# Attention scores: the low part of the queries in both halves of a tile

## The chip, the cores and the metric

The kernel runs on one core of a Trainium2 chip. The metric is the device time of one launch in microseconds. The kernel before takes 2771.27 us, the median of 3 runs (2769.14 to 2774.12).

Five engines work side by side, each through its own instructions in order, and wait for each other by semaphores: TensorE (PE; the load of its stationary operand stands in the profile as an engine of its own, PEld), VectorE (DVE), ScalarE (ACT), GpSimd (POOL) and SyncE (SP). PE writes to PSUM, the others work on SBUF and PSUM.

## What is computed

Two layers of a model over 512 latent and 256 context tokens of width 1024. In each layer a normed input goes through one projection and then through three mixers side by side (neighbourhood attention, a gated delta rule, a Fourier transform), whose results are gated, merged and projected; an MLP follows. The change lies in the attention, 8 heads of width 64:

```python
s_loc = (jnp.einsum('bwhd,biwjhd->bhwij', q_r, k_win).astype(jnp.float32)
         + jnp.transpose(bias, (0, 2, 1, 3)).astype(jnp.float32)[None])
s_ctx = jnp.einsum('bwhd,bshd->bhws', q_r, kc).astype(jnp.float32)
s = jnp.concatenate([s_loc.reshape(b, h, GRID_W, kh * kw), s_ctx], axis=-1)
p = jax.nn.softmax(s, axis=-1).astype(v.dtype)
...
return (jnp.einsum('bhwij,biwjhd->bwhd', p_loc, v_win)
        + jnp.einsum('bhws,bshd->bwhd', p[..., kh * kw:], vc))
```

In layer 0 the context tokens attend to each other as well.

## The kernel before

**Tiling.** Activations lie feature-major, 128 features on the partitions and up to 768 tokens along them. Products are made of two float32r parts each: a weight or an activation is its rounded part (`hi`) plus the remainder (`lo`), and `proj` (L240) adds up hi x hi, hi x lo and lo x hi over eight groups of 128 features, in pieces of 512 and 256 tokens. Weights come from memory by `wload` (L225): SP issues the transfer, ACT rounds, POOL or DVE makes the remainder.

**Attention.** Heads are treated in pairs, since two heads of 64 features fill 128 partitions. `na_in` (L745) makes three projections for a pair. Of the keys it keeps, for each head, a tile `ks` whose one half holds the rounded part of the head's keys and whose other half holds their remainder (L753 to L756). Of the queries it makes, for each head, a tile `qd` with the rounded part in both halves (ACT writes the one, DVE the other, L778 and L779), and for both heads one tile `qlo` with the remainder, each head in its own half (DVE, L780).

`na_attn` (L823) goes over the query tiles of a pair, 128 queries each: four local ones and, in layer 0, two of the context. `score` (L826) makes the scores of one head by two products into one PSUM bank: L829 takes `qd` against `ks` over 128 rows (rounded queries with both parts of the keys), L830 takes `qlo` against the rounded keys, over the 64 rows of that head. A local tile has 256 local and 256 context keys; its local keys are one piece of 256 columns, and two of 128 columns in the first tile. So a pair has 22 products with `qlo` in layer 0 and 18 in layer 1, and the kernel 160.

`na_pair` (L784) does the rest for both heads: DVE takes the maximum and adds the bias (L793, L796), ACT takes the exponentials (L800, L803), DVE divides (L807), PE transposes the weights (L812), ACT copies them (L813), and PE multiplies by the values (L818).

**Order.** Within the stage of the mixers four streams are emitted side by side by clocks of their own (`by_clock`, L330): the scan of the delta rule (`dn_step`), its preparation (`dn_prep`, with a chain of 31 x 2 small DVE steps, L581 and L583, that inverts blocks), the attention, and the projections with the gates (`stream_in`). A scheduler then sets each engine's order from the order of emission, as priority, and from an estimate of when each operand is there. The order is fixed in the program: on the chip an engine waits at an instruction whose operands are late, and all behind it waits too. Projections are what PE does between the steps of the other streams.

**Room.** The tiles of a stage lie in pools, each tag with a number of buffers in rotation. `ks`, `qd`, `qlo`, the values and the output share the tag `n` with 7 buffers, as many as one pair uses (L1044).

Of the kernel before, what the change touches and what calls it, by code (L numbers as in the profile page):

```python
# [9 lines left out]
F32 = mybir.dt.float32  # L10
# [17 lines left out]
# n-tiles of w_in, 128 columns each  # L28
T_NAK, T_NAV, T_NAQ, T_DNK, T_DNV, T_DNQ, T_Z, T_U, T_GATE = 0, 4, 8, 12, 16, 20, 24, 28, 32
# PSUM buffers of the mixers; buffers of the raw and of the split weights  # L30
PSX = {"pl": 2, "pa": 1, "ch": 2, "s": 2, "pp": 1}
WRAW, WSPLIT, WADA = 4, 3, 8
# order in which the streams of the mixers are emitted, for each layer: the share of the clock that a projection and
# a step of the scan take, the lead and the priority of the scan, the gates per projection and those ahead of it
IN_T, LAT_STEP, HEAD, PRI, GR, G0 = (12, 7), (2, 3), (5, 0), (200, 0), (0.5, 0.3), (0, 1)
# rows of adaLN tiles per projection, and how far their loads run ahead
ADA_RATE, ADA_LAG = 0.6, 1
# gates computed beside the mixers
NPRE = 16
# columns of the vector block  # L40
# [4 lines left out]
def kernel(ctx: ExitStack, tc: tile.TileContext, A: dict, out: bass.AP):  # L45
# [75 lines left out]
    def sigmoid_into(dst, src):  # L121
        """exp(min(x, 0) - log(1 + exp(-|x|))); dst is not src"""
        act.activation(out=dst, in_=src, func=AF.Abs)
        act.activation(out=dst, in_=dst, func=AF.Exp, scale=-1.0)
        act.activation(out=dst, in_=dst, func=AF.Ln, bias=1.0)
        dve.scalar_tensor_tensor(dst, in0=src, scalar=0.0, in1=dst, op0=ALU.min, op1=ALU.subtract)
        act.activation(out=dst, in_=dst, func=AF.Exp)

# [9 lines left out]
    def ada_block(l, q):  # L138
        """columns 512*q .. 512*q+511 of the adaLN projection of layer l, the contraction in four column groups"""
# [16 lines left out]
    def ada_group(l, q, lag):  # L156
        """four such blocks from the one at q, one in each column group; loads run lag rows of tiles ahead"""
# [26 lines left out]
    def ada_scale(l, i, k0=0, n=KD):  # L184
        """norm weight * (1 + scale) of the norm i of layer l"""
# [27 lines left out]
    def ada_upto(l, q):  # L213
        """what follows needs the block q of layer l"""
# [8 lines left out]
    wcnt = [0]  # L223

    def wload(src, kn=KD):  # L225
        """[P, kn, 128] float32 -> for each k two float32r parts whose sum is the float32 one"""
# [13 lines left out]
    def proj(ps, w, kn, xh, xl, segs, off=0, k0=0, k1=KD):  # L240
        """ps[:, seg - off] = sum_k w[:, k].T @ x[k][:, seg], of it the part from k0 to k1"""
# [6 lines left out]
    def split_act(src, w, name, alloc):  # L248
        """float32 SBUF tile -> (hi, lo) tiles"""
# [7 lines left out]
    class Rms:  # L257
        """1 / rms of each token; the last of the tiles goes straight to the sum over partitions"""
# [33 lines left out]
    def mod_norm(l, i, xs, w, nm):  # L292
        """the modulated norm as two parts"""
# [24 lines left out]
    def modulate(k, x):  # L318
        """the first modulation, of a normalised tile that is no longer needed"""
# [10 lines left out]
    def by_clock(pri, *streams):  # L330
        """merge generators that yield the time of what they have emitted, by their clocks"""
# [33 lines left out]
    def layer(l):  # L365
# [39 lines left out]
        def gates():  # L405
# [40 lines left out]
            # rows of the summed log-decays, for a broadcast over partitions  # L446
# [7 lines left out]
        odn = drp.tile([NDH, P, TT], F32, tag="odn", bufs=1, name="odn")  # L454

        def conv_silu(ps, cw, w):
            """short conv over tokens and silu; the result at [0:512] and [514:770]"""
# [41 lines left out]
        def tok_major(src, offs, name, tag):  # L499
            """[feature, token] -> [token, 6, feature]"""  # L500
# [23 lines left out]
        def dn_prep(h, st):  # L524
# [41 lines left out]
            # inverses of the 32x32 diagonal blocks, one block on each partition  # L566
# [28 lines left out]
            # merge 32 -> 64  # L595
# [23 lines left out]
            # merge 64 -> 128  # L619
# [26 lines left out]
        def dn_step(h, st, d, step):  # L646
            """one chunk of the scan of direction d"""
# [95 lines left out]
        ona = drp.tile([4, P, TT], F32, tag="ona", bufs=1, name="ona")  # L743

        def na_in(c, st):  # L745
            # scores as products of two parts each: the two halves of a stack hold the parts of one head
# [26 lines left out]
            if full:  # L773
                act.activation(out=raw[:, TL:TT], in_=ps[1][:, 0:TC], func=AF.Copy, scale=0.125)
            qd = [U("qd", F32R, tag="n") for _ in range(2)]
            qlo = U("qlo", F32R, tag="n")
            for t, r, r2 in zip(qd, halves, halves[::-1]):
                act.copy(t[r, :W], raw[r, :W])  # L778
                dve.tensor_copy(t[r2, :W], raw[r, :W])  # L779
                dve.tensor_tensor(qlo[r, :W], raw[r, :W], t[r, :W].bitcast(F32), op=ALU.subtract)  # L780
            st.update(ks=ks, vt=vt, qd=qd, qlo=qlo)
            yield IN_T[l]

        def na_pair(scores, n_loc, biases, vts, dst, view):  # L784
            """softmax over the keys of 128 queries for both heads of a pair; the outputs to dst, feature-major"""
# [37 lines left out]
        def na_attn(c, st):  # L823
            vt = st["vt"]

            def score(ps, hh, q0, k0, n):  # L826
                r = slice(64 * hh, 64 * hh + 64)
                q, k = slice(q0, q0 + P), slice(k0, k0 + n)
                pe.matmul(ps, lhsT=st["qd"][hh][:, q], rhs=st["ks"][hh][:, k], start=True, stop=False)  # L829
                pe.matmul(ps, lhsT=st["qlo"][r, q], rhs=st["ks"][hh][r, k], start=False, stop=True)  # L830
# [40 lines left out]
        ofn = drp.tile([4, P, TT], F32, tag="ofn", bufs=1, name="ofn")  # L871

        def fourier():
# [34 lines left out]
            for i, (s0, n, tab) in enumerate(sets):  # L908
# [24 lines left out]
                for g in range(4):  # L933
# [9 lines left out]
                    else:  # L943
                        # the transform at (n - t, -f) is the one at (t, f); -f lies 64 rows away, but for 0 and 64
# [36 lines left out]
        def stream_na():  # L981
            for c, st in enumerate(nas):
                while "qlo" not in st:
# [60 lines left out]
        mix_b = scope("mixb", n=7, N=1, PT=2, L=1, pr=3, sp=7, S=3, s6=6, Pm=2, bias=2, stmp=1)  # L1044
# [67 lines left out]
        for hb in range(4):  # L1112
# [12 lines left out]
            for k in range(KD):  # L1125
# [3 lines left out]
                # the last one in halves of the tokens, so that the final norm starts early  # L1129
# [165 lines left out]
```

## Time and profile before

| | |
|---|---|
| time, median of 3 runs | 2771.27 us |
| span of the profiled execution, first to last instruction | 2750.2 us |
| time around the span (median less span) | 21.1 us |
| PE busy | 2618.0 us, 95% |
| DVE busy | 1391.2 us, 51% |
| ACT busy | 1191.1 us, 43% |
| mixers of layer 0 | 145 to 772 us of the span |
| mixers of layer 1 | 1687 to 2218 us of the span |

The profiled execution is one run; its own time is not listed apart from its span, so the median less the span is taken for what lies around it. The busy time of an engine is the union of its instructions' intervals. PE's products are pipelined and their intervals overlap, so the step of PE's work is read from one start to the next, not from the durations.

### The profile page before, as it was taken

To read this page: it belongs to the slowest core of one execution; us is meant where nothing else is said; L and a number is where in the kernel's file an instruction comes from. 1 tells how busy PE (TensorE), PEld (TensorE's weight loads), DVE (VectorE), ACT (ScalarE), POOL (GpSimd) and SP (SyncE) were. 2 spreads that over 40 slices of the span, in tenths; PEclk is the share of its full clock that TensorE was granted. 3 is DMA by queue.
4 is the path that set the end of the run, shared out by engine and by line. 5 is a ranking of instruction groups with operands and counts; after the bars stand their busy time and mean duration, and the time that the engine had idled before them with its cause. 6 is when DMAs were issued, how large, how long until landed. Compare 5 with 4: busy or idle time off the path is not lost.

```text
span 2750.2 us, 40072 instructions
## 1 busy us (share of the span) xinstructions
PE 2618.0 (95%) x15066; PEld 2103.9 (77%) x15066; DVE 1391.2 (51%) x2831; ACT 1191.1 (43%) x2430; POOL 609.1 (22%) x522
## 2 busy tenths in 40 slices
PE   6999999999999999999999988998999999999998
PEld 3877768677878777888888867776777777788886
DVE  5657576857423634222222365768677436433334
ACT  4546555555543224121222255455565654423333
POOL 3222212231111112111111123221323222222222
PEclk9999999999999999999999999999999999999999
DMA  6232222221255743342312223232232335333332
GB/s 219 81 87 68 78 58 75 71 71 53 68 197 189 255 139 115 104 135 91 120 59 66 81 60 111 72 81 58 79 85 63 93 112 187 96 95 96 96 96 88
DMA packets 196705, 278.41 MB, mean 101 GB/s; under 512 B 56768, under 2 KB 75936, under 8 KB 196512
## 3 DMA queue, kind: packets, MB, share of 16 engines
q1 hardware_dynamic: 196512, 275.87, 32.9%
q8 instruction: 118, 1.93, 0.3%
q14 instruction: 75, 0.61, 0.1%
HBM read 244.29 MB, written 27.31 MB: 99 GB/s over the span
## 4 chain that ended last, share of the span: by engine, by line
PE 73%; DVE 8%; ACT 3%; DMA 1%; issue 1%; POOL 1%; SPq 0%; DVEq 0%; ACTq 0%; POOLq 0%
PE ps_m L245 32%; PE ps_in L245 14%; PE ps_br L245 6%; PE ps_wo L245 4%; PE ps_inc L245 3%; PE ps_ada L168 1%; DVE cy L468 1%; PE ps_s L830 1%; PE ps_s L818 1%; PE ps_s L829 1%; PE ps_s L812 1%; DVE xn L303 1%; PE ps_ch L676 1%; DVE stmp L581 1%; DMA Db<-gdr 1%
## 5 line engine op out<-in xcount | busy, mean ns | idle before, releaser
L236 POOL TENSOR_TENSOR wlo<-wr,whi 128x512 fp32r<-128x512 f32 x360 | 484.8, 1348 | 1894.7 <-ACT whi L233 1789.7
L233 ACT CAST whi<-wr 128x512 fp32r<-128x512 f32 x560 | 346.3, 619 | 879.9 <-PE ps_m L245 519.8
L245 PE MATMUL ps_in<-hh,whi 128*128 128x512 f32 x960 | 381.0, 408 | 11.8 <-ACT kraw L750 5.5
L245 PE MATMUL ps_in<-hh,wlo 128*128 128x512 f32 x960 | 378.2, 404 | 2.2 <-POOL wlo L236 2.2
L245 PE MATMUL ps_in<-hl,whi 128*128 128x512 f32 x960 | 377.7, 404 | 0.0
L236 DVE TENSOR_TENSOR wlo<-wr,whi 128x512 fp32r<-128x512 f32 x200 | 138.6, 693 | 244.7 <-ACT whi L233 243.9
L245 PE MATMUL ps_m<-ml,whi 128*128 128x512 f32 (+1 forms) x768 | 233.8, 358 | 4.1 <-POOL ml L313 3.2
L245 PE MATMUL ps_m<-mh,whi 128*128 128x512 f32 (+1 forms) x768 | 233.0, 358 | 2.9 <-ACT mh L309 2.9
L245 PE MATMUL ps_m<-ah,wlo 128*128 128x512 f32 (+1 forms) x776 | 234.4, 355 | 0.0
L245 PE MATMUL ps_m<-ah,whi 128*128 128x512 f32 (+1 forms) x776 | 234.2, 355 | 0.0
L245 PE MATMUL ps_m<-al,whi 128*128 128x512 f32 (+1 forms) x776 | 233.2, 353 | 0.0
L245 PE MATMUL ps_m<-mh,wlo 128*128 128x512 f32 (+1 forms) x768 | 231.7, 355 | 0.0
L245 PEld LDWEIGHTS ps_in<-hh,whi 128*128 128x128 f32 x960 | 181.8, 194 | 48.1 <-ACT kraw L750 5.9
L245 PEld LDWEIGHTS ps_in<-hh,wlo 128*128 128x128 f32 x960 | 181.2, 193 | 36.5 <-POOL wlo L236 3.4
L245 PEld LDWEIGHTS ps_in<-hl,whi 128*128 128x128 f32 x960 | 181.4, 194 | 32.8 <-issue 2.0
L1134 DVE SCALAR_TENSOR_TENSOR x<-ps_m,mod,x 128x512 f32<-128x512 f32 (+1 forms) x97 | 60.8, 655 | 247.8 <-PE ps_m L245 247.8
L245 PEld LDWEIGHTS ps_m<-mh,whi 128*128 128x128 f32 x768 | 126.6, 189 | 35.3 <-ACT whi L233 8.4
L245 PEld LDWEIGHTS ps_m<-ah,whi 128*128 128x128 f32 x776 | 127.7, 188 | 28.9 <-ACT whi L233 6.7
L245 PE MATMUL ps_inc<-hh,whi 128*128 128x256 f32 x512 | 149.6, 292 | 0.0
L245 PEld LDWEIGHTS ps_m<-ml,whi 128*128 128x128 f32 x768 | 126.8, 188 | 29.5 <-POOL ml L313 6.0
L245 PE MATMUL ps_inc<-hl,whi 128*128 128x256 f32 x512 | 148.7, 290 | 0.0
L245 PE MATMUL ps_inc<-hh,wlo 128*128 128x256 f32 x512 | 147.0, 287 | 0.0
(325 smaller groups left out, 4927.3 us busy)
## 6 DMA issues: line engine op xcount, KB each, us to landing
wr<-in_w_dram SPq DMA_DIRECT2D x256, 256.0 KB
wr<-in_wi_dram SPq DMA_DIRECT2D x224, 256.0 KB
wada<-in_wa_dram SPq DMA_DIRECT2D x192, 256.0 KB
wr<-in_wb_dram SPq DMA_DIRECT2D x48, 256.0 KB
wr<-in_wo_dram SPq DMA_DIRECT2D x32, 256.0 KB
gpre<-sgp SPq DMA_DIRECT2D x16, 384.0 KB
sgg<-gpre SPq DMA_DIRECT2D x16, 384.0 KB
rot<-kn SPq DMA_DIRECT2D x64, 64.0 KB
```

The costliest lines, as they stand in the source:

```text
L168: pe.matmul(ps[32 * j:32 * j + 32, :], lhsT=cs[:, k, :], rhs=ws[k][j], start=(k == 0), stop=(k == KD - 1), tile_position=(0, 32 * j))
L233: act.copy(hi, raw)
L236: eng.tensor_tensor(lo, raw, hi.bitcast(F32), op=ALU.subtract)
L245: pe.matmul(ps[:, s0 - off:s1 - off], lhsT=a, rhs=b[k][:, s0:s1], start=(k == 0 and i == 0), stop=(k == kn - 1 and i == 2))
L303: dve.scalar_tensor_tensor(t[:, s0:s1], in0=xs[k][:, s0:s1], scalar=sc, in1=rs[:, s0:s1], op0=ALU.mult, op1=ALU.mult)
L468: dve.scalar_tensor_tensor(y[:, :n], in0=cin[:, j:j + n], scalar=vec[:, cw + j:cw + j + 1], in1=y[:, :n], op0=ALU.mult, op1=ALU.add)
L581: dve.tensor_tensor(tv, Nb[:, j + 1:32, j:j + 1].to_broadcast([48, n, m]), Wb[:, j:j + 1, 0:m].to_broadcast([48, n, m]), op=ALU.mult)
L676: pe.matmul(ps[:, 2 * P:3 * P], lhsT=kt, rhs=Uc, start=True, stop=True)
L812: pe.transpose(ps[:, i * P:(i + 1) * P], Pm[:, i * P:(i + 1) * P], ident)
L818: pe.matmul(pss[0][f, 0:P], lhsT=v[:, f], rhs=Pt[:, i * P:(i + 1) * P], start=(i == 0), stop=(i == nk // P - 1), tile_position=(0, 64 * hh))
L829: pe.matmul(ps, lhsT=st["qd"][hh][:, q], rhs=st["ks"][hh][:, k], start=True, stop=False)
L1134: dve.scalar_tensor_tensor(x2[k][:, s0:s1], in0=ps[:, s0:s1], scalar=mod(l, 5, k, v), in1=x2[k][:, s0:s1], op0=ALU.mult, op1=ALU.add)
```

## The change

`qlo` is replaced by two tiles `ql`, one for each head, that hold the remainder of the head's queries in both halves. DVE makes both halves by a subtraction each. The second score product then runs over 128 rows like the first: remainder of the queries against both parts of the keys. So it also adds the product of the two remainders, which was left out before. The tag `n` gets an eighth buffer, and the space for descriptors of dynamic transfers is set to 2048 bytes. Comments are removed, which moves the line numbers.

```diff
             qd = [U("qd", F32R, tag="n") for _ in range(2)]
-            qlo = U("qlo", F32R, tag="n")
-            for t, r, r2 in zip(qd, halves, halves[::-1]):
+            ql = [U("ql", F32R, tag="n") for _ in range(2)]
+            for t, lo, r, r2 in zip(qd, ql, halves, halves[::-1]):
                 act.copy(t[r, :W], raw[r, :W])
                 dve.tensor_copy(t[r2, :W], raw[r, :W])
-                dve.tensor_tensor(qlo[r, :W], raw[r, :W], t[r, :W].bitcast(F32), op=ALU.subtract)
-            st.update(ks=ks, vt=vt, qd=qd, qlo=qlo)
+                for x in (r, r2):
+                    dve.tensor_tensor(lo[x, :W], raw[r, :W], t[r, :W].bitcast(F32), op=ALU.subtract)
+            st.update(ks=ks, vt=vt, qd=qd, ql=ql)
...
             def score(ps, hh, q0, k0, n):
-                r = slice(64 * hh, 64 * hh + 64)
                 q, k = slice(q0, q0 + P), slice(k0, k0 + n)
                 pe.matmul(ps, lhsT=st["qd"][hh][:, q], rhs=st["ks"][hh][:, k], start=True, stop=False)
-                pe.matmul(ps, lhsT=st["qlo"][r, q], rhs=st["ks"][hh][r, k], start=False, stop=True)
+                pe.matmul(ps, lhsT=st["ql"][hh][:, q], rhs=st["ks"][hh][:, k], start=False, stop=True)
...
-        mix_b = scope("mixb", n=7, N=1, PT=2, L=1, pr=3, sp=7, S=3, s6=6, Pm=2, bias=2, stmp=1)
+        mix_b = scope("mixb", n=8, N=1, PT=2, L=1, pr=3, sp=7, S=3, s6=6, Pm=2, bias=2, stmp=1)
...
-    nc = _bacc.Bacc("TRN2", target_bir_lowering=False, num_devices=1)
+    nc = _bacc.Bacc("TRN2", target_bir_lowering=False, num_devices=1, dynamic_dma_scratch_size=2048)
```

The counts of instructions stay the same but for DVE, which gets 16 more. The scheduler sets another order in the stage of the mixers. Three places of it follow; in brackets stand the engines whose semaphores an instruction waits for.

DVE, layer 0, first head pair, from the copy of the first head's queries on (`stmp` and `Wb` belong to the inverse of the blocks in `dn_prep`, `s` to the softmax), before:

```order
L779 CAST qd<-qraw 64x768 [waits Activation_49]
L583 TENSOR_TENSOR Wb<-Wb,stmp 48x22x10 [waits DVE_49]
L780 TENSOR_TENSOR qlo<-qraw,qd 64x768 [waits Activation_49]
L581 TENSOR_TENSOR stmp<-Nb,Wb 48x231 [waits DVE_49]
L779 CAST qd<-qraw 64x768
L583 TENSOR_TENSOR Wb<-Wb,stmp 48x21x11 [waits DVE_49]
L780 TENSOR_TENSOR qlo<-qraw,qd 64x768 [waits Activation_49]
L581 TENSOR_TENSOR stmp<-Nb,Wb 48x240 [waits DVE_49]
L793 TENSOR_REDUCE s_1870<-ps_s 128x1 [waits PE_49]
```

The same place now:

```order
L780 CAST qd<-qraw 64x768 [waits Activation_49]
L583 TENSOR_TENSOR Wb<-Wb,stmp 48x22x10 [waits DVE_49]
L782 TENSOR_TENSOR ql<-qraw,qd 64x768 [waits Activation_49]
L581 TENSOR_TENSOR stmp<-Nb,Wb 48x231 [waits DVE_49]
L782 TENSOR_TENSOR ql<-qraw,qd 64x768
L583 TENSOR_TENSOR Wb<-Wb,stmp 48x21x11 [waits DVE_49]
L780 CAST qd<-qraw 64x768
L581 TENSOR_TENSOR stmp<-Nb,Wb 48x240 [waits DVE_49]
L782 TENSOR_TENSOR ql<-qraw,qd 64x768 [waits Activation_49]
L583 TENSOR_TENSOR Wb<-Wb,stmp 48x20x12 [waits DVE_49]
L782 TENSOR_TENSOR ql<-qraw,qd 64x768
```

Each head has two subtractions in place of one, and the first reduction of the softmax stands two rows further down than the last one shown.

PE, the same pair, from the first score product to the first with the remainder (`ps_s` holds scores, `ps_in` a projection), before:

```order
L829 MATMUL ps_s<-ks,qd 128x128 [waits DVE_49,Activation_49]
L245 MATMUL ps_in<-hh,wlo 128x512
L245 MATMUL ps_in<-hh,whi 128x512
L245 MATMUL ps_in<-hl,whi 128x512
L245 MATMUL ps_in<-hh,wlo 128x512
L830 MATMUL ps_s<-ks,qlo 128x128 [waits DVE_49]
```

The same place now:

```order
L830 MATMUL ps_s<-ks,qd 128x128 [waits DVE_49,Activation_49]
L245 MATMUL ps_in<-hh,wlo 128x512
L245 MATMUL ps_in<-hh,whi 128x512
L245 MATMUL ps_in<-hl,whi 128x512
L245 MATMUL ps_in<-hh,wlo 128x512
L245 MATMUL ps_in<-hh,whi 128x512
L245 MATMUL ps_in<-hl,whi 128x512
L245 MATMUL ps_in<-hh,wlo 128x512 [waits Pool_49]
L245 MATMUL ps_in<-hh,whi 128x512
L245 MATMUL ps_in<-hl,whi 128x512
L831 MATMUL ps_s<-ks,ql 128x128 [waits DVE_49]
```

Nine projection products stand between the two score products, where four stood.

PE, layer 0, third head pair, last local query tile, around the transposes of the softmax (`Pm` holds its result, `ps_l` the norms of keys in `l2_rope`), before; above the first row shown stand 29 more projection products, and above these the scores:

```order
L245 MATMUL ps_inc<-hh,whi 128x256
L245 MATMUL ps_inc<-hl,whi 128x256
L245 MATMUL ps_inc<-hh,wlo 128x256
L812 MATMUL ps_s<-ident,Pm 128x128 [waits DVE_49,Activation_49]
L812 MATMUL ps_s<-ident,Pm 128x128 x3
L812 MATMUL ps_s<-ident,Pm 128x128 [waits DVE_49,Activation_49]
```

The same place now, from the last score product on:

```order
L831 MATMUL ps_s<-ks,ql 128x256
L482 MATMUL ps_l_5223<-r_l_5221,ones 128x512 [waits Activation_49]
L814 MATMUL ps_s<-ident,Pm 128x128 [waits DVE_49,Activation_49]
L482 MATMUL ps_l_5227<-r_l_5221,ones 128x256 [waits Activation_49]
L814 MATMUL ps_s<-ident,Pm 128x128 x3
L814 MATMUL ps_s<-ident,Pm 128x128 [waits DVE_49,Activation_49]
```

The 32 projection products that stood between the scores and the transposes now stand ahead of the scores.

## Rows read from the trace of the kernel before

**Rows 1.** The page: PE's and DVE's busy times, and PE in 40 slices.
```profile
PE 2618.0 (95%) x15066; PEld 2103.9 (77%) x15066; DVE 1391.2 (51%) x2831; ACT 1191.1 (43%) x2430; POOL 609.1 (22%) x522
...
PE   6999999999999999999999988998999999999998
```

**Rows 2.** Busy us by stretch: stretch, length, PE, PEld, DVE, ACT, POOL; then PEclk.
```profile
145.00:772.00 627.00, 595.73 (x3972) 481.91 (x3971) 402.29 (x1045) 345.18 (x793) 146.56 (x126) 0.98 0.25 73
1687.00:2218.00 531.00, 492.78 (x3101) 384.78 (x3100) 354.67 (x935) 295.10 (x692) 144.06 (x126) 0.95 0.28 80
```

**Rows 3.** Timeline of PE, layer 0: start, duration (us), engine, line, operation, rows*columns, shape.
```profile
204.56 0.39 PE L245 MATMUL ps_in<-hh,wlo 128*128 128x512 f32 x1
204.79 0.28 PE L245 MATMUL ps_inc<-hh,whi 128*128 128x256 f32 x1
204.90 0.28 PE L245 MATMUL ps_inc<-hl,whi 128*128 128x256 f32 x1
...
210.82 0.38 PE L829 MATMUL ps_s<-ks,qd 128*128 128x256 f32 x1
211.13 0.38 PE L830 MATMUL ps_s<-ks,qlo 64*128 64x256 f32 x1
211.44 0.39 PE L829 MATMUL ps_s<-ks,qd 128*128 128x256 f32 x1
211.76 0.38 PE L830 MATMUL ps_s<-ks,qlo 64*128 64x256 f32 x1
212.07 0.50 PE L245 MATMUL ps_in<-hh,wlo 128*128 128x512 f32 x1
212.41 0.39 PE L245 MATMUL ps_in<-hh,whi 128*128 128x512 f32 x1
```

**Rows 4.** Line L830, its products and weight loads: duration in ns (min/median/max), forms.
```profile
L830 PEld LDWEIGHTS ps_s<-ks,qlo x144: 182/183/285, 198.8 to 2147.3; 64*128 64x128 f32 x144
L830 PE MATMUL ps_s<-ks,qlo x144: 322/380/579, 198.8 to 2147.3; 64*128 64x256 f32 x112, 64*128 64x128 f32 x32
...
L830 PE MATMUL ps_sc<-ks,qlo x16: 379/381/386, 246.9 to 685.3; 64*128 64x256 f32 x16
```

**Rows 5.** Timeline of PE, layer 0, first pair, first query tile.
```profile
199.08 0.33 PE L829 MATMUL ps_s<-ks,qd 128*128 128x128 f32 x1
199.34 0.32 PE L830 MATMUL ps_s<-ks,qlo 64*128 64x128 f32 x1
199.59 0.39 PE L829 MATMUL ps_s<-ks,qd 128*128 128x256 f32 x1
```

**Rows 6.** Groups of DVE by line and shape, L780: count, busy us, mean ns, idle before.
```profile
L780 DVE TENSOR_TENSOR qlo<-qraw,qd 64x768 fp32r<-64x768 f32 x8 | 7.6, 952 | 0.2
L780 DVE TENSOR_TENSOR qlo<-qraw,qd 64x512 fp32r<-64x512 f32 x8 | 5.5, 682 | 0.1
```

**Rows 7.** Timeline of DVE, layer 0, first pair: one small step of the block inverse.
```profile
198.68 0.39 DVE L581 TENSOR_TENSOR stmp<-Nb,Wb 48x231 f32<-48x231 f32 x1
```

**Rows 8.** Waits of PE, longest first: us in total, times, longest.
```profile
PE ps_s L812 <- DVE Pm L807: 16.1, 14, 5.2
```

**Rows 9.** Timeline of PE: scores and transposes of two tiles; waits in brackets.
```profile
524.15 0.38 PE L830 MATMUL ps_s<-ks,qlo 64*128 64x256 f32 x1
...
530.78 0.63 PE L812 MATMUL ps_s<-ident,Pm 128*128 128x128 f32 x4
...
533.06 0.63 PE L812 MATMUL ps_s<-ident,Pm 128*128 128x128 f32 x4 [1.65 <-DVE Pm L807]
...
1889.48 0.38 PE L830 MATMUL ps_s<-ks,qlo 64*128 64x256 f32 x1
...
1898.87 0.44 PE L812 MATMUL ps_s<-ident,Pm 128*128 128x128 f32 x1 [5.17 <-DVE Pm L807]
```

**Rows 10.** Busy time by stretch, layer 0, second pair; PEclk is the granted clock.
```profile
336.00:339.40 3.40, 3.15 (x12) 2.00 (x12) 3.21 (x6) 0.22 (x1) 0.00 (x0) 1.00 0.79 203
339.40:346.20 6.80, 6.80 (x19) 5.14 (x19) 4.48 (x20) 2.11 (x8) 0.00 (x0) 0.50 0.05 9
```

More of the change, by code (lines that the diff above doesn't have):

```diff
@@ L982, in stream_na @@
             for c, st in enumerate(nas):
-                while "qlo" not in st:
+                while "ql" not in st:
                     yield 2
```

## The prediction

> **What bounds the kernel now.** I read the page's busy times first. TensorE (PE) is busy for 95% of the span, VectorE (DVE) for 51%, and in the 40 slices PE stands at 9 almost everywhere [rows 1]. Then I cut out the two stretches in which attention scores are computed, the mixer stage of each layer. There PE is busy 595.7 of 627 us and 492.8 of 531 us [rows 2], so it waits 31 and 38 us, and what bounds both stages is the in-order queue of PE. A microsecond of PE work that goes away shortens the program, unless PE then waits for something else.
>
> The third view is PE's timeline, read by the distance from one start to the next, since the listed durations overlap. A projection product over 512 columns is followed after 0.23 us, one over 256 columns after 0.11 to 0.12 us [rows 3]. The score products over 256 columns lie in the same rows: qd at 210.82, qlo at 211.13, qd at 211.44, qlo at 211.76, the next projection at 212.07. Each step is 0.31 us, whether a 128-row product follows a 64-row one or the other way round. The first projection behind them is late too: 0.34 us to its successor in place of 0.23 [rows 3]. What is paid extra, 0.19 us, is about one weight load (183 ns) [rows 4]. The loads of full-row products are as long, and in the projections they are hidden. So the reading is: at each change between 128 and 64 rows the next weight load isn't hidden behind the running product. The 64-row qlo product costs two such changes.
>
> **The change, part by part.**
>
> *Both score products over 128 rows.* No product is added or taken away: 144 + 16 with qlo become 144 + 16 with ql [rows 4]. Of the 160, 32 are over 128 columns and 128 over 256.
> - 128 products over 256 columns: 0.19 us going in and 0.19 us coming out, 128 x 0.38 = 48.6 us.
> - 32 over 128 columns (first query tile): the steps there are 0.25 to 0.26 us [rows 5]. With no change of rows I put 0.11 us, the step that 256 columns need at most, so 32 x 0.29 = 9.2 us. Fewer columns may step faster, for some 3 us more; I leave that out.
> - In 40 places of the trace a 512-column projection follows the last qlo, as at 212.07; its successor is 0.11 us late: 4.4 us.
>
> Together 62 us of PE time, 34 us in layer 0 (88 products) and 28 us in layer 1 (72).
>
> [...]
>
> *Eight times two more subtractions on DVE.* A subtraction takes 952 ns in layer 0 and 682 ns in layer 1 [rows 6]: 8 x 0.95 + 8 x 0.68 = 13 us of DVE time, in stages where DVE is busy 402 of 627 and 355 of 531 us [rows 2]. It isn't PE's time, but the first ql product waits for it, and the order shows what stands behind: the second head's copy, its subtractions, then the first reduction of the softmax. The scheduler has put nine projection products ahead of the first ql in place of four ahead of the first qlo. Nine cover 9 x 0.23 = 2.1 us. From the first qd on, DVE needs two subtractions and the two small steps of the block inverse that stand ahead of and between them, at 0.39 us each [rows 7]: 0.95 + 0.95 + 0.8 = 2.7 us. So PE waits some 0.6 us there; on the second head it is again two subtractions, a copy and steps between, against 7 x 0.23 + 4 x 0.12 = 2.1 us of projections and the five score products, now short. I take 0.75 us for each of the eight head pairs, 6 us, between 0 (the scheduler's cover is enough) and 8 x 1.6 = 13 us (both subtractions bare).
>
> *Softmax behind faster scores.* Each of the 40 query tiles runs scores, softmax on DVE and ScalarE (ACT), transposes on PE. PE works on projections in the meantime, and the wait for the softmax is already its largest in attention, 16.1 us in 14 places [rows 8]. The second head's scores were part of the cover, and they shrink by 0.75 us. The scheduler has also moved projections. For each tile I took the time from head 0's last score to the end of its softmax in the trace and set it against what now stands between in the order. Three tiles lose nearly all cover:
> - layer 0, third pair, last local tile. Before, head 0's last score started at 524.15 and the transposes at 530.78, over four scores and 32 projections (4.7 us), and the second head's transposes waited 1.65 us [rows 9]. Now only the second head's four scores and a product of the norm stand between, some 0.8 us. Wait about 6 us in place of 1.65, so 4.3 us more.
> - layer 0, first pair, same tile: 4.3 us of projections shrink to 0.9 us; 3.5 us more.
> - layer 1, second pair, third tile: it waits 5.17 us [rows 9] behind 20 projections of 0.12 us; these have gone ahead of the scores, so 2.4 + 0.8 = 3.2 us more.
>
> The other 37 tiles, by the same subtraction, add 25 us, 36 us in all. That is an upper bound: the softmax times of before hold DVE's own queueing behind other work (9.4 us from score to transposes in the layer 1 tile, 6.6 us in the layer 0 one [rows 9]), and projections that left one gap fill another. Lower bound 0. I take half, 18 us.
>
> *The clock.* [...] I take 3 us gained, and bounds of 5 gained and 0.
>
> *The rest.* One more tile buffer fits since the scratch of the DMA queues is made smaller; every tag keeps its rotation, and no transfer is added. The order of the other streams moves by less than one projection. Cost nothing; the cover is that all DMAs here are issued by SP, which the change doesn't lengthen.
>
> Sum: -62 + 6 + 18 - 3 = -41 us. The profiled execution has a span of 2750.2 us, 21.1 us less than the median of 2771.27 us; what lies around the span doesn't change. Span 2709 us, time 2730 us.
>
> **The rivals.**
> - *Nearly all of it arrives.* The moved projections cover the softmax, and a wait at one place only shortens the next. For it: PE waits just 69 us of the two stages now. Time 2771 - 62 - 5 + 5 = 2709 us or so.
> - *The waits take it all.* Softmax and ql waits reach their bounds (36 + 13 us) and other chains through DVE (the scan, the norms of keys and queries) lose their cover likewise, 10 us more: -62 + 59 = -3, 2768 us, no difference. Against it: these bounds count every tile at its worst.
> - *Slower, by one mechanism: the transposes stand too close behind the scores.* It decides from 62 / 40 = 1.55 us of new wait per tile. If each lost 2 us, +80 - 62 = +18 us, 2789 us. Against it: of 40 tiles only three lose more than 3 us of projections by my count, and total cover falls from 208 to 200 us.
> - *The change of rows isn't what costs.* If the steps of 0.31 us came from loading a new stationary tile at every score product, whatever its rows, the 128-row pairs would step as now, and DVE's 6 us remain, 13 at most: 2771 + 6 = 2777 us, up to 2784. Against it: the projections also load at every product and step by 0.12 us [rows 3]. [...]
>
> **How the numbers follow.** Forecast 0.77, nearly all 0.12, waits take it 0.05, transposes slower 0.03, rows not the cause 0.03. Low end: -62 - 5 = -67 us, 2704 us. High end: -62 + 36 + 8 = -18 us, 2753 us (the softmax at its bound and ql somewhat above my value). A measurement of this kernel can tell 0.2%, 5.5 us, from no change. Faster: 0.77 + 0.12 = 0.89; same: 0.05 and half of the last rival, 0.07; slower 0.04.
>
> **What would show it.** In the profile after, a qd and ql block of four should take some 0.5 us of PE in place of 1.25, all loads at 128 rows. PE's busy time in the mixer stages should fall by about 60 us. The wait of the transposes for the softmax should grow from 16 us to some 34 us, with new ones at the three tiles named; ql should appear among PE's waits with some 6 us. Steps of 0.31 us between qd and ql would make the prediction wrong at its root; stages shortened by PE busy time but filled with waits of 60 us would make it wrong at the cover.

## The result and the profile after

The kernel now takes 2734.7 us, the median of 4 runs (2732.88 to 2736.07), against 2770.91 us for the kernel before in the same set (4 runs, 2769.14 to 2774.12): a ratio of 0.9868, 95% interval 0.9851 to 0.9885. Run again later beside 17 runs of the kernel before (median 2763.29 us), it took 2736.71 us: 0.9898 (0.988 to 0.9916). So the change gains 27 to 36 us; 41 us were forecast.

The page of the kernel after, span, busy times and PE in 40 slices, the answer to [rows 1]:

```profile
span 2731.1 us, 40072 instructions
...
PE 2567.2 (94%) x15066; PEld 2083.0 (76%) x15066; DVE 1405.7 (51%) x2847; ACT 1191.6 (44%) x2430; POOL 619.5 (23%) x522
...
PE   6998989899999999999999988898999999999998
```

The span is 19.1 us shorter than the profiled one of before. PE's busy time falls by 50.8 us, from 2618.0 to 2567.2, and PE's time without work grows from 132.2 to 163.9 us, by 31.7. DVE gets 14.5 us more. So two thirds of the work that PE lost has come back as waiting, in this pair of executions.

Both stages of the mixers by stretch, columns as in [rows 2]:

```profile
147.00:764.00 617.00, 570.85 (x3974) 474.70 (x3973) 410.24 (x1053) 345.34 (x793) 144.38 (x126) 0.98 0.25 74
1680.00:2199.00 519.00, 464.63 (x3096) 368.85 (x3094) 360.91 (x942) 294.53 (x692) 156.11 (x126) 0.97 0.29 81
```

They are 10 and 12 us shorter. PE's busy time in them goes from 1088.5 to 1035.5 us, and the time in which PE waits from 31 and 38 us to 46 and 54.

PE's timeline in a block of score products of layer 0, in the columns of [rows 3]:

```profile
216.97 0.39 PE L830 MATMUL ps_s<-ks,qd 128*128 128x256 f32 x1
217.19 0.28 PE L831 MATMUL ps_s<-ks,ql 128*128 128x256 f32 x1
217.31 0.29 PE L830 MATMUL ps_s<-ks,qd 128*128 128x256 f32 x1
217.43 0.28 PE L831 MATMUL ps_s<-ks,ql 128*128 128x256 f32 x1
217.55 0.39 PE L245 MATMUL ps_in<-hh,whi 128*128 128x512 f32 x1
217.78 0.28 PE L830 MATMUL ps_s<-ks,qd 128*128 128x256 f32 x1
```

The steps between the score products are 0.12 us, but for the first with 0.22, where [rows 3] has 0.31, and the projection behind them is followed after 0.23 us, not 0.34. The four products hold PE for 0.58 us in place of 1.25. The line of the second product shows that all its loads are full, and no shorter for it (columns as in [rows 4]):

```profile
L831 PEld LDWEIGHTS ps_s<-ks,ql x144: 186/189/193, 201.4 to 2128.2; 128*128 128x128 f32 x144
L831 PE MATMUL ps_s<-ks,ql x144: 270/281/363, 201.4 to 2128.4; 128*128 128x256 f32 x112, 128*128 128x128 f32 x32
```

A load of 0.19 us stands in front of every product, and the products start every 0.12 us: the loads are hidden. In the kernel before, with loads nearly as long (0.18 us [rows 4]) and steps of 0.31 us [rows 3], it is the change of rows that uncovers the load.

That it is the change, and not the 64 rows, another place in the trace of before bears out, where twelve products over 64 rows and 64 columns follow each other:

```profile
253.06 0.91 PE L625 MATMUL ps_r<-Tst,N 64*64 64x64 f32 x12
```

They start every 0.058 us, though the loads (L625) last 0.13 us each; only on the way into such a run of products is the step long, 0.33 us behind a projection over 512 columns where 0.23 is usual.

Where the waiting went is in PE's list of waits (us in total, times, longest), after:

```profile
PE ps_s L814 <- DVE Pm L809: 26.8, 21, 6.4
...
PE ps_l L482 <- ACT r_l L477: 14.2, 9, 4.0
PE ps_tm L505 <- DVE kT L496: 10.0, 5, 3.0
...
PE ps_kk L556 <- DVE qT L496: 7.0, 3, 3.5
PE ps_s L831 <- DVE ql L782: 4.9, 10, 0.8
PE ps_s L814 <- ACT Pm L805: 4.8, 2, 4.1
```

The same list of the kernel before has these rows beside the one in [rows 8]:

```profile
PE ps_l L482 <- ACT r_l L477: 9.1, 9, 2.2
...
PE ps_tm L505 <- DVE kT L496: 7.0, 5, 3.0
...
PE ps_kk L556 <- DVE qT L496: 3.5, 2, 2.8
```

The transposes' wait for the softmax grows from 16.1 us to 26.8 + 4.8 (the second row is the same instruction, released by ACT). The wait for `ql` is new, 4.9 us. Three chains that the change doesn't touch, the norms (`ps_l`) and two products of the delta rule's preparation, wait 14.2 + 10.0 + 7.0 us where they waited 9.1 + 7.0 + 3.5. The sum is 15.5 + 4.9 + 11.6 = 32 us, which is what PE's time without work has grown by.

### The profile page after: what moved, and what is told of

It reads as the page before. It is cut to its first block, busy times and chain, and to the rows that moved or that the text cites. A ratio compares the mean times of both kernels' runs of the same rounds, so it can differ in the third digit from the quotient of the medians.

```text
span 2731.1 us, 40072 instructions
## 1 busy us (share of the span) xinstructions
PE 2567.2 (94%) x15066; PEld 2083.0 (76%) x15066; DVE 1405.7 (51%) x2847; ACT 1191.6 (44%) x2430; POOL 619.5 (23%) x522
## 5 line engine op out<-in xcount | busy, mean ns | idle before, releaser
L236 POOL TENSOR_TENSOR wlo<-wr,whi 128x512 fp32r<-128x512 f32 x360 | 496.3, 1380 | 1849.8 <-ACT whi L233 1725.3
L245 PE MATMUL ps_in<-hh,wlo 128*128 128x512 f32 x960 | 372.6, 399 | 0.8 <-POOL wlo L236 0.8
L245 PE MATMUL ps_in<-hl,whi 128*128 128x512 f32 x960 | 371.1, 397 | 0.0
```

The costliest lines, as they stand in the source:

```text
L236: eng.tensor_tensor(lo, raw, hi.bitcast(F32), op=ALU.subtract)
L245: pe.matmul(ps[:, s0 - off:s1 - off], lhsT=a, rhs=b[k][:, s0:s1], start=(k == 0 and i == 0), stop=(k == kn - 1 and i == 2))
```

## The experiments

Each kernel's ratio is to the kernel before, whose runs were made beside it on the same chip; where two experiments are compared by microseconds, they ran in the same set unless said otherwise. The sets are e1 to e4, e5 to e8, and e9 with e10. The scheduler sets an order anew for each kernel; where it matters, the text says how far the order is that of another.

**Was the profiled execution of before a typical one?** The span of 2750.2 us lay 21 us under the median, and the prediction put this down to time around the span. e1 is the kernel before with one comment shortened. e2 is the kernel before with the one line of the change that makes the scratch smaller:

```diff
-    nc = _bacc.Bacc("TRN2", target_bir_lowering=False, num_devices=1)
+    nc = _bacc.Bacc("TRN2", target_bir_lowering=False, num_devices=1, dynamic_dma_scratch_size=2048)
```

> The kernel before, one comment shortened. After the change the time fell by 36 us but the profiled span by 19 us only. Theory A, time around the span: 21 us lie around the span of the kernel before and 2 us around that of the changed one, so here the time is 2771 us, the span 2750 us, 21 us apart. Theory B, the profiled execution of before was a quicker one than its timed runs: time 2771 us, span of the timed runs 2769 us, 2 us apart, and the mixer stages are longer in this trace than in the first one by some 17 us.

> The kernel before with the space for dynamic transfers set to 2048 bytes, nothing else. Theory A (that space costs time outside the span): 2771 - 17 = 2754 us, span as before. Theory B (it costs nothing, the score products make all 36 us): 2771 us within 3 us, ratio 1.000.

e1: 2766.43 us (2756.1 to 2774.57, 12 runs), ratio 0.9994 (0.9973 to 1.0014). Its profiled execution took 2767.38 us, and span and mean granted clock of it are

```profile
core 0: 2765.3 us, clock 0.977
```

So 2.1 us lie around the span, not 21, and the profiled execution of before was a quick one, some 15 us under the usual, at a granted clock of 0.981. The mixers of e1, from 147 to 780 and from 1700 to 2236 us, are 11 us longer than in that trace, where theory B wanted some 17. e2: 2765.68 us, 0.9997 (0.9978 to 1.0016); the scratch gives and takes nothing.

The runs of before beside e1 to e10, 64 in all, show what goes with it. Time and mean granted clock move together, from 2752.7 us at 0.983 to 2778.7 at 0.970; a straight line through them falls by 21 us for each 0.01 of clock. At 0.9815, the mean clock of the change's 10 runs, it gives 2754.3 us. So of the 27 to 36 us, some 18 remain at equal clock (2754.3 less their median of 2736.3), about what the two profiled executions, 0.981 and 0.982, differ by; the rest goes with a clock that is 0.0055 higher than the 0.976 that before has in the mean, 0.0055 x 2120 = 12 us by the line. The line alone doesn't say which is cause and which effect.

**Do the rows make the gain, and what does the work on DVE cost?** e3 keeps the text of the change and takes the second product over 64 rows again; its order is not quite the change's (in layer 0's first pair, four projections and not nine stand between the first two score products). e4 is the kernel before with the second product over 128 rows, from `qd` a second time, so that nothing is added on DVE and PE doesn't wait for a remainder (the scratch as in the change). e7 is the kernel before, with the one tile `qlo` read over all 128 rows: the other half of it holds the other head's remainder, and meets there the remainder of the keys.

```diff
e3, from the kernel after
+                r = slice(64 * hh, 64 * hh + 64)
-                pe.matmul(ps, lhsT=st["ql"][hh][:, q], rhs=st["ks"][hh][:, k], start=False, stop=True)
+                pe.matmul(ps, lhsT=st["ql"][hh][r, q], rhs=st["ks"][hh][r, k], start=False, stop=True)
e4, from the kernel before
-                pe.matmul(ps, lhsT=st["qlo"][r, q], rhs=st["ks"][hh][r, k], start=False, stop=True)
+                pe.matmul(ps, lhsT=st["qd"][hh][:, q], rhs=st["ks"][hh][:, k], start=False, stop=True)
e7, from the kernel before
-                pe.matmul(ps, lhsT=st["qlo"][r, q], rhs=st["ks"][hh][r, k], start=False, stop=True)
+                pe.matmul(ps, lhsT=st["qlo"][:, q], rhs=st["ks"][hh][:, k], start=False, stop=True)
```

> The changed kernel, with ql made in both halves on DVE and the eighth buffer, but the second score product again over the 64 rows of its head. The output is complete. Theory C (the change of rows is what the gain comes from): slower than the changed kernel by 36 us or more, 2771 to 2784 us, steps of 0.31 us between qd and ql. Rival (the new order or the buffers make the gain): 2735 to 2745 us.

e3: 2770.1 us (2757.9 to 2782.89, 12 runs), 1.0013 (0.9993 to 1.0034). The gain is gone, all of it, and the steps of before are back; PE's timeline of e3, layer 0:

```profile
216.82 0.38 PE L830 MATMUL ps_s<-ks,qd 128*128 128x256 f32 x1
217.13 0.38 PE L832 MATMUL ps_s<-ks,ql 64*128 64x256 f32 x1
217.44 0.39 PE L830 MATMUL ps_s<-ks,qd 128*128 128x256 f32 x1
217.76 0.38 PE L832 MATMUL ps_s<-ks,ql 64*128 64x256 f32 x1
```

0.31 us from start to start, with the operands of the change. With the slow products in place the added work on DVE costs 4 us over e1, which is within the measurement. That the rows do it without any part of the order, e10 below shows for 112 of the 160 products.

> The kernel before with the smaller scratch, whose second score product takes qd over 128 rows a second time in place of qlo over 64; the remainder of the queries is left out of the scores, DVE makes it as before and nobody reads it. So it has the rows of the change without DVE's 13 us and without the wait for ql. Theory C: steps of 0.12 us; 2735 - 5 (PE's wait for ql) - up to 6 (softmax starting earlier) = 2724 to 2730 us. Rival (waits of the softmax alone eat the gain, ql nothing): 2735 us as the changed kernel.

e4: 2721.88 us (2713.82 to 2722.39, 4 runs), 0.9824 (0.9799 to 0.9849), 45 us under the kernel before and a little under what was expected.

> The kernel before, whose second score product takes the one tile qlo over all 128 rows: its other half holds the other head's remainder, which meets the remainder of the head's keys. That adds to each score a product of two remainders of different heads, where the changed kernel adds that of the same head. DVE's work, the buffers and the scratch are as before; the first score of either head now waits for both heads' remainders. Theory E (DVE's second subtraction costs the changed kernel 13 us, as the kernel with qd twice showed): 2722 to 2728 us. Rival (qd twice was quicker because it waits for no remainder at all): 2735 us.

e7: 2720.89 us (2719.74 to 2725.03, 5 runs), 0.9843 (0.9823 to 0.9864): 42 us under the kernel before and 16 us under the change. It beats both, with nothing of what the change adds on DVE: one tile `qlo` for both heads with 7 buffers as before, one subtraction for each head, the scratch untouched. PE's waits in e7:

```profile
PE ps_s L812 <- DVE Pm L807: 31.6, 24, 5.8
...
PE ps_l L482 <- ACT r_l L477: 7.6, 7, 2.2
```

Nothing waits for `qlo` on PE, and the norms wait 7.6 us, not 14.2; the softmax is waited for about as long as in the change (31.6 and, released by ACT, 3.5 against 26.8 + 4.8). The two profiled spans, 2722.9 and 2731.1 us at one clock of 0.982, differ by 8 us of the 16. So what the change adds beside the rows, which costs nothing to be measured while the scores are slow (e3), costs 8 to 16 us once they are fast. The likely reading is that the cover of the added subtractions was the work that the change removes. It is not shown alone: e7's order is neither that of before nor that of the change.

**Does the gain follow the number of products?** e5 is the change once more, for a measure in this set; e6 puts the second products with the context's keys back to 64 rows. Its trace counts 64 + 16 = 80 of 160; the expectation says 88.

```diff
e6, from the kernel after
+                r = slice(64 * hh, 64 * hh + 64) if k0 >= TL else slice(0, P)
-                pe.matmul(ps, lhsT=st["ql"][hh][:, q], rhs=st["ks"][hh][:, k], start=False, stop=True)
+                pe.matmul(ps, lhsT=st["ql"][hh][r, q], rhs=st["ks"][hh][r, k], start=False, stop=True)
```

> The changed kernel, an empty line added, in more rounds and beside the next three. Theory D (of the 36 us, some 21 come from PE's queue and some 14 from a higher granted clock, since the kernel before has many executions with a low clock): 2735 us, the clocks of the executions around 0.981 where the kernel before has 0.975, and at an equal clock the two kernels lie 21 us apart. Rival (the four executions so far happened to have a high clock): clocks as before, time 2745 us.

> The changed kernel with the second score product over the head's 64 rows again where the keys are those of the context (88 of 160), over 128 rows elsewhere. The output is complete. Theory C (each change of rows costs, so the gain goes by their count): 88 of 160 changes are back, 2735 + 0.55 x 35 = 2754 us, clock between the two kernels. Rival (one change per tile costs as much as three, for PE is waited for anyway): 2765 to 2770 us.

e5: 2736.71 us (2734.43 to 2737.04, 6 runs), 0.9898, within 2 us of the first measure. e6: 2745.37 us (2739.51 to 2757.01, 6 runs), 0.9935 (0.9911 to 0.9959). It lies between the change and the kernel before, nearer to the change than expected: half of the products back, in the order of the change, and 8.7 of 26.6 us lost. Its runs spread over 17 us; their mean clock of 0.981 is the change's, so the 8.7 us are rather to be set against the 18 at equal clock, and are about half of them.

**Could POOL take the second half?** In e8 the second of the two subtractions goes to POOL, which is busy 23% of the span.

```diff
e8, from the kernel after
-                for x in (r, r2):
-                    dve.tensor_tensor(lo[x, :W], raw[r, :W], t[r, :W].bitcast(F32), op=ALU.subtract)
+                for e, x in ((dve, r), (pool, r2)):
+                    e.tensor_tensor(lo[x, :W], raw[r, :W], t[r, :W].bitcast(F32), op=ALU.subtract)
```

> The changed kernel with the subtraction into the second half made by POOL in place of DVE. The output is complete. Theory E: DVE's queue is as before, POOL's subtraction of 64x768 takes some 2 us beside it, so the remainder comes no later than by two subtractions on DVE, and the softmax behind no longer waits for them: 2724 to 2733 us. Rival (POOL's subtraction delays the weights that POOL makes, or is later than DVE's): 2735 to 2745 us.

e8: 2753.59 us (2749.88 to 2759.63, 12 runs), 0.9964 (0.995 to 0.9978): 17 us worse than the change, and well off what was expected. The groups by line and shape (count, busy us, mean ns, idle before), in the change:

```profile
L782 DVE TENSOR_TENSOR ql<-qraw,qd 64x768 fp32r<-64x768 f32 x16 | 15.2, 952 | 0.4
...
L780 DVE CAST qd<-qraw 64x768 fp32r<-64x768 f32 x8 | 7.4, 923 | 7.2 <-ACT qraw L774 7.0
```

and the same on DVE and POOL in e8:

```profile
L780 DVE CAST qd<-qraw 64x768 fp32r<-64x768 f32 x8 | 11.8, 1481 | 7.4 <-ACT qraw L774 7.2
L782 DVE TENSOR_TENSOR ql<-qraw,qd 64x768 fp32r<-64x768 f32 x8 | 10.6, 1327 | 0.2
...
L782 POOL TENSOR_TENSOR ql<-qraw,qd 64x768 fp32r<-64x768 f32 x8 | 16.5, 2065 | 0.6
```

POOL needs 2.07 us for what DVE does in 0.95, and DVE's own copy and subtraction beside it become slower, 0.92 to 1.48 and 0.95 to 1.33 us. The longest of DVE's subtractions takes 2456 ns in e8, against 956 in the change. Why they become longer beside POOL's is not shown. PE waits for both:

```profile
PE ps_s L830 <- DVE qd L780: 13.6, 12, 3.5
PE ps_s L831 <- DVE ql L782: 11.8, 11, 3.3
```

25.4 us, where the change waits 4.9 us for `ql` and 4.7 for `qd`. But the 17 us that e8 loses are not the price of POOL alone. With one subtraction for each head left on DVE, the scheduler came back to the order of before: PE, DVE and ACT run the same sequence of operations and tiles as there, so four projections and not nine stand ahead of the first product with `ql`. And PE's time without work is only 7 us longer than in e5 (171.8 against 165.1 us), while PE's busy time, for the same products, is 9 us longer (2579.4 against 2570.1): the clock is lower (0.975 against 0.981 in the mean), as the next section shows.

**Where does the clock come from?** In the kernel before the granted clock falls from 1.00 to 0.50 near the first query tiles [rows 10]; the change's trace has no such stretch there. Theory F puts this down to the first tile, where PE waits for the queries and the products are short, rival G to the number of 64-row products, wherever they stand. e9 puts the second products of the first tile alone (48) back to 64 rows, e10 those of all other tiles (112).

```diff
e9, from the kernel after
+                r = slice(64 * hh, 64 * hh + 64) if q0 == 0 else slice(0, P)
e10, from the kernel after
+                r = slice(64 * hh, 64 * hh + 64) if q0 > 0 else slice(0, P)
both
-                pe.matmul(ps, lhsT=st["ql"][hh][:, q], rhs=st["ks"][hh][:, k], start=False, stop=True)
+                pe.matmul(ps, lhsT=st["ql"][hh][r, q], rhs=st["ks"][hh][r, k], start=False, stop=True)
```

> The changed kernel with the second score product over 64 rows in the first query tile of each head pair alone (48 products: 32 over 128 columns, 16 over 256), over 128 rows in all other tiles. The output is complete. [...] Rival G (the clock goes by the number of 64-row products, wherever they stand): 48 of 160, 2736 + 0.3 x 30 = 2745 us, the clock in between.

> The counterpart: 64 rows in all tiles but the first of each pair (112 products over 256 columns), 128 rows in the first. The output is complete. Theory F: the clock stays high near the first tiles, clock 0.981; the rows alone cost 112 x 0.38 = 43 us of PE's steps, of which at the ratio of the whole change (18 of 62 at an equal clock) 12 to 20 us are seen: 2748 to 2756 us. Rival G: 112 of 160, the clock near that of before, 2736 + 0.7 x 30 = 2757 us with low clock near the first tiles too.

e9: 2746.7 us (2742.05 to 2757.8, 7 runs), 0.9934 (0.9911 to 0.9957). e10: 2763.09 us (2754.63 to 2770.73, 12 runs), 0.9988 (0.9971 to 1.0005). Over the change as e5 measured it that is 10 and 26 us. The first 12 us of first tiles by stretch (columns as in [rows 2]; the granted clock is the third from the end), in the change, layer 0's first pair:

```profile
199.00:211.00 12.00, 10.30 (x59) 8.31 (x60) 11.75 (x29) 4.46 (x13) 2.26 (x2) 1.00 0.06 22
```

in e9, layer 0's first pair and layer 1's first:

```profile
200.00:212.00 12.00, 12.00 (x34) 8.46 (x34) 9.17 (x22) 0.95 (x2) 0.00 (x0) 0.57 0.06 21
...
1750.00:1762.00 12.00, 11.98 (x33) 8.23 (x34) 8.92 (x29) 1.33 (x5) 0.00 (x0) 0.57 0.05 16
```

in e10, layer 0's first pair:

```profile
199.00:211.00 12.00, 10.31 (x58) 8.32 (x59) 11.75 (x29) 4.35 (x13) 2.15 (x2) 1.00 0.08 26
```

and in e8 of the last section, whose score products all have 128 rows, layer 0's first pair and layer 1's first:

```profile
201.00:213.00 12.00, 10.60 (x51) 9.04 (x52) 11.03 (x30) 3.25 (x11) 2.27 (x5) 0.72 0.01 2
...
1749.00:1761.00 12.00, 11.51 (x60) 10.43 (x60) 11.54 (x39) 4.39 (x12) 0.27 (x1) 0.75 0.00 1
```

In the same 12 us PE does 59 products in the change, 58 in e10 and 34 in e9, where its clock is 0.57 in the mean. In the trace of e9, 27.3 us near three of the eight first tiles are at a clock of 0.50, as many as in that of before, and none in e10 or in the change. So filling the rows of the first tile took these stretches away. But 64 rows there are neither needed for them nor enough. In e8 the clock falls near all eight first tiles, to 0.72 to 0.86 in the mean of such stretches of 12 us, of which PE is busy for 8.3 to 11.5 us, and is low for 37.5 us in all; in the trace of before, layer 0's first pair has no such stretch. Nor are all the low stretches gone with the change: by the traces' records of the granted clock it has 97 us at 0.50 in all and the kernel before 107. A new one of 10 us, at 242 us of the span, begins during PE's wait for the norms in the first pair's last local tile:

```profile
239.46 0.28 PE L831 MATMUL ps_s<-ks,ql 128*128 128x256 f32 x1
243.25 2.07 PE L482 MATMUL ps_l<-r_l,ones 128*128 128x512 f32 x2 [3.51 <-ACT r_l L477]
```

What the low clock costs has to be read on one execution at a time. The profiled execution of e9 is the slowest of its seven, 2757.8 us; it has 144.5 us at 0.50 where that of e5 has 101.5. At 0.50 a projection over 512 columns is followed after 0.43 us, at 1.00 after 0.23 (kernel before, 342.25 to 344.81 us and [rows 3]), so about half of the time at 0.50 is lost. Half of the difference is 21 us, by these numbers an estimate of what the low clock costs, and 21 us is what it took longer than e5's 2736.96. For e8 (139.5 us at 0.50) half of the difference is 19 us, and it took 16 longer. So in these two the clock's share is as large as the whole loss. e10 is the other case. It has the change's order, row for row on PE, DVE and ACT, and it has 108.6 us at 0.50, which by the same estimate is 4 us of the 25 that its execution took longer. The pages of e5 and e10 say where the rest lies:

```profile
PE 2570.1 (94%) x15066; PEld 2085.8 (76%) x15066; DVE 1402.9 (51%) x2847; ACT 1191.7 (44%) x2430; POOL 620.9 (23%) x522
...
PE 2614.2 (95%) x15066; PEld 2101.9 (76%) x15066; DVE 1402.3 (51%) x2847; ACT 1191.5 (43%) x2430; POOL 617.4 (22%) x522
```

PE's busy time is 44 us longer, where 112 x 0.38 = 43 us of steps were expected (some 4 us of it may be the clock's), and PE's time without work 19 us shorter (145.9 against 165.1 us): part of what the rows cost is given back as waits that are then shorter. With nothing but the rows changed, this is the plainest proof that they make the gain. By their medians, e9's time is what rival G put and its stretches lie where theory F has them, and e10 is slower than either had it; the two losses, 10 and 26 us, exceed the gain of 27 to 30 us that the change shows in the later sets. In e10's trace the clock was low for 20.5 us at 259 us of the span; why one execution has such long stretches and another hasn't stays open.

## Why the prediction was right, and where not

The time forecast, 2730 us, is 5 us from the result, which lies inside the range. The mechanism of the main term was right, and so was the wait for `ql`. That the time came out so close is luck: on the two traces that the sum is about, the spans differ by 19.1 us and not by 41, and the 22 us that the forecast span of 2709 us was too short were made up by 19 us too much around it.

- *Score products, -62 us.* The steps came out as put, 0.58 us for a block of four where 0.5 was forecast, and e3 and e10 show that the rows make the gain. PE's busy time fell by 53 us in the mixers, not by some 60. The likely reason, argued and not tested: a product lasts 0.28 us and the next starts after 0.12, so the last one ahead of a wait counts some 0.16 us more than its step, and there are more such waits now.
- *Waits for `ql`, +6 us.* 4.9 us, in 10 places of at most 0.8 us each. The direct wait was right. What the second tile costs in all is not 6 but 8 to 16 us, by e7 (its order included).
- *Softmax, +18 us.* The transposes' waits grew by 15.5 us; half of the upper bound, taken without a reason, happened to fit. Of the three tiles that were named, the one of layer 0's first pair waits 3.51 us, as shown above (3.5 more were forecast), at the norms. The one of the third pair reads in PE's timeline:

```profile
526.58 0.28 PE L831 MATMUL ps_s<-ks,ql 128*128 128x256 f32 x1
530.86 1.15 PE L482 MATMUL ps_l<-r_l,ones 128*128 128x512 f32 x2 [3.99 <-ACT r_l L477]
532.81 0.45 PE L814 MATMUL ps_s<-ident,Pm 128*128 128x128 f32 x1 [0.80 <-ACT r_l L483]
```

PE waits 3.99 + 0.80 us there (forecast 6, before 1.65 [rows 9]), but it waits at the product of the norms that stands ahead of the transposes, and so the list has it under `ps_l` and not under the softmax. So 7.5 us of the norms' 14.2 stand in tiles that the prediction had under the softmax, and the line between this term and the last one is not sharp. The layer 1 tile reads

```profile
1878.64 0.28 PE L831 MATMUL ps_s<-ks,ql 128*128 128x256 f32 x1
...
1885.82 0.45 PE L814 MATMUL ps_s<-ident,Pm 128*128 128x128 f32 x1 [6.43 <-DVE Pm L809]
```

PE waits 6.43 us, 1.3 more than in [rows 9] where 3.2 more were forecast. From head 0's last score, the first row, to the transposes it is 7.2 us, where [rows 9] has 9.4. DVE got through its chain sooner: before, it stood idle in it for 0.78 us on ACT, and L126 and L805 took 1.40 and 1.22 us, where the same two steps now take 0.95 and 0.14. So the softmax times of before were no fixed cost, the reason for which the sum over all tiles was taken as an upper bound.
- *The rest, nothing: this step failed.* "The order of the other streams moves by less than one projection. Cost nothing". The norms and the two products of the delta rule's preparation wait 11.6 us longer. The likely reason is that the projections that covered them stand elsewhere and PE comes to them sooner; the order shows it for the norms in the third pair of layer 0, where 32 projections have gone. The rival in which the waits take it all had this term, at 10 us; it belonged into the sum.
- *The clock, -3 us: near for the trace, mis-sized for the usual execution.* No run shows a term of 3 us. In its place the two traces show that 107 us at 0.50 became 97, which by the estimate of half is 5 us: all the low stretches at the first tiles are gone, but others came or grew, as the one of 10 us at 242 us, which begins during PE's wait of 3.51 us, and the one at 532 us, 6.8 us long where the kernel before has 3.4 at 534 us. But the trace was of a quick execution; the one of e1 has 44 us at its first tiles and 127 in all. By the line over 64 runs the higher clock goes with some 12 us.
- *What lies around the span, 21 us: a wrong reading.* It is 2 us. The sum was laid on a quick execution and 21 us added back, which made up for a gain put at twice its size there. The true account is other than the one I wrote: some 18 us at equal clock and 9 to 18 by the clock, in place of 38 and 3. Close agreement of the total hides that the first is half the size and the second several times.

The four rivals: that the rows don't matter is excluded by e3 and e10. That all of it arrives is what e4 and e7 do (42 to 45 us gained), where nothing is added on DVE. That waits take it all was half true. Slower transposes did not come: only a few of the 40 tiles wait 2 us more or longer.

What stays open is how e7's lead divides between the wait for `ql` (4.9 us), the norms' and other products' places in PE's order (6.6 us at `ps_l`) and the clock, since all go at once, and what sets the long stretches of low clock. Whether POOL would serve in the order of the change is open too, for e8 has another.

## What to carry to other kernels

In a stream of PE products over 128 rows, a single product over 64 cost two uncovered weight loads here (0.19 us each): try to fill it up to 128 rows with what already lies in the other half, as e7 does, before making a second copy for it. What the filling adds must be small enough to stand in the result; here it is a product of two remainders, of different heads in e7. Each microsecond taken from the engine that sets the end was also somebody's cover; so count the waits of chains that the change doesn't touch, and ask of each operation that is added whether its cover is the very work that goes away. Before a sum is laid on one profiled execution, set its span and granted clock against the other runs: here it lay 15 us under the usual. And before two variants are compared, set their orders against each other: moving one operation to POOL brought back another order on three engines.

## What the runs showed of the chip

- One program on one core gave times from 2752.7 to 2778.7 us over 64 runs, 0.9%, in step with the mean granted clock (0.983 to 0.970). The change and e4, e7 spread less (2732.88 to 2737.04 us over the change's 10 runs, 2713.82 to 2722.39 in e4, 2719.74 to 2725.03 in e7), and the change's trace has no low stretch near the first tiles (clock 1.00 in all eight stretches of 12 us); e10's has none there either (1.00), and its runs spread over 16 us.
- The price of a change of rows depends on the two products that meet: in steps of 256 columns it is 0.19 us each way, and a 512-column product behind it is 0.11 us late [rows 3]. Products over 64 rows and 64 columns that follow each other step by 0.058 us (L625).
- By the recorded spans a 64x768 subtraction takes POOL 2.07 us and DVE 0.95, and the subtraction and the copy that DVE makes beside it become 40 to 60% longer in the mean (1.33 for 0.95, 1.48 for 0.92 us).
